# Gate and first feed-forward products of a decoder step in Strassen's form (Winograd's variant, one level)

## The chip, the cores and the metric

One core of one Trainium2 chip runs the whole program in one launch. The metric is the device time of that launch in microseconds (us). Before the change three runs gave 1571.78, 1574.46 and 1579.22 us; the median is 1574.46.

## The reference, cut to what matters

Two decoder layers are computed for 512 prompt tokens and 32 sample tokens together (544 columns, NT). In each layer, after the mixers and their output projection, this follows (D = 1024, inner width 4096):

```python
h = layer_norm(ALPHA * h + mix, ln1_g, ln1_b)
ff = jnp.square(jax.nn.relu(h @ w_ff1)) @ w_ff2
ple = jax.nn.sigmoid(h @ w_ple_gate) * (pe @ w_ple_proj)
h = layer_norm(ALPHA * h + ff + ple, ln2_g, ln2_b)
```

Everything is float32 at the interface. The change touches `h @ w_ple_gate` and `h @ w_ff1` and what lies around them.

## The kernel before, in words

**Numbers.** Each float32 operand of a large product is split into two parts of the format fp32r: `hi` is the operand rounded (a cast on ScalarE), `lo` is the operand less `hi` (a subtraction on VectorE or GpSimd). A product is then three matmuls per 128x128 weight block, weight-hi by x-hi, weight-lo by x-hi and weight-hi by x-lo (`mm3`; all matmuls have the one line L620).

**Tiling.** Activations are kept transposed: 8 blocks of 128 channels by 544 columns, in two halves of 288 and 256 columns (HALF). A gate or first-layer product of one output block (a "chunk" of weights, 128x1024 float32, 512 KB) is 2 halves x 8 blocks x 3 = 48 matmuls. The gate has 8 such chunks in a layer, the first feed-forward product (f1) 32, the second one (f2) 32.

**Order of the feed-forward part** (`backbone`): output projection `w_o` (second half of its contraction per column half), the projection `w_p`, the gate, then twice (kh = 0, 1): 16 chunks of f1 whose squared-ReLU results stay on chip as hi and lo, and 8 output blocks of f2 over those 16. The residual is added from the hi and lo parts of h in `evac_f2` (L1734, L1736).

**Weights on their way.** SyncE's queue loads a chunk into one of 2 `raw` buffers (L591); `splits` casts it to `hi` on ScalarE (L603) and makes `lo` on VectorE, for some chunks on GpSimd (L607); there are 4 `hi` and 4 `lo` buffers, freed when the chunk's products are issued.

**LayerNorm.** `ln_apply` adds sums over the channels by matmuls, works out mean and inverse root in a chain of small VectorE operations (L654), broadcasts both by matmuls and spawns `ln_col` for each of 8 blocks: two VectorE operations that read PSUM (L740, L742), a scale and bias on ScalarE (L748), the cast (L753) and GpSimd's subtraction (L755).

**Evacuation of f1** (`evac_f1`): ReLU on ScalarE (L1712), square on GpSimd (L1715), cast on ScalarE (L1717), lo on VectorE (L1719).

**Planner.** The program is written by generators ("streams") that a small planner, `Sched`, runs while the program is built: every step carries an engine and a charge in ns (`cP`, `cV`, `cA`, `cS`, `cG` for TensorE, VectorE, ScalarE, GpSimd), every buffer and event a planned time, and at each point the step with the earliest planned start, less its stream's priority (`PR`), is issued. An `Alt` lets the planner take the engine that ends earlier. So the order on each engine is fixed when the program is built. The chip runs each engine's list in order.

Of the kernel before, what the change touches and what calls it, by code (L numbers as in the profile page):

```python
# [23 lines left out]
T = 4  # L24
# [24 lines left out]
PR = {'q_sample': -1.5, 'free_raw': 7, 'gmix': 1.0, 'evac_c1': 10.5, 's_scores': 13.0, 's_block': 8.5, 'mix_b': 4.5, 'load_r': 6.5, 'kidx': 10.5, 's_attn': 14, 'evac_au': 6.5, 'head': 8.0, 's_kt': 10.0, 'loads': 1.5, 'evac_q': 0.0, 'sgu_load': 7.5, 's_relu': 12.5, 'mix_a': 13, 'setup1': 9.0, 's_attn_f': 8.5, 'gmlp': 7.5, 'unit': 8.0, 'load_pe': 14, 'evac_oa': 8, 'backbone': -2, 'evac_c0': -1.5, 'setup2': -2, 'splits': 7.5, 's_qk': 0.5, 'gnorm': 7.0, 'store': 11, 'setup': 3.0}  # L49
# [31 lines left out]
class Sched:  # L81
    def __init__(self, pools, caps):
# [6 lines left out]
        self.n = 0  # L89

# [24 lines left out]
    def run(self):  # L115
        while self.streams:
# [27 lines left out]
            for s in self.streams:  # L144
                if isinstance(s.item, (list, Alt)):
                    opts = s.item.opts if isinstance(s.item, Alt) else (s.item,)
                    bo = None
                    for i, o in enumerate(opts):
                        e, c = o[0]
                        st = max(s.ready + hop(s.e, e), self.eng.get(e, 0.0))  # L150
                        if bo is None or st + c + BIAS < bo[0]:
                            bo = (st + c, st - (WP if e == "P" else WO) * s.prio, i)
# [25 lines left out]
def cP(n, k=1):  # L178
    return ("P", max(n / 2.4 + 2.5, 107.0) * k)
# [193 lines left out]
def build(tc, I, O, cols):  # L373
# [4 lines left out]
    caps = {"Ah": 1, "Al": 1, "Bh": 1, "Bl": 1, "w": 5, "raw": 2, "hi": 4, "lo": 4, "u": 23, "t": 11, "mm": 2, "at": 6}  # L378
# [4 lines left out]
    S = Sched(pools, dict(caps, lk=1, un=UN))  # L383
# [142 lines left out]
    chunks = []  # L526

    def chunk(src, f, g=False, native=False, s=False, cut=()):
# [5 lines left out]
        chunks.append(c)  # L534
        return c

    W = []
    for l in range(L):
# [10 lines left out]
        w["g"] = [chunk(I["w_g"][l, c, 0], 1024, c < 2) for c in range(8)]  # L549
        w["f1"], w["f2"] = [None] * 32, [[None] * 4 for _ in range(8)]  # L550
        for kh in range(2):
            for c in range(16):
                w["f1"][kh * 16 + c] = chunk(I["w_f1"][l, kh * 16 + c, 0], 1024)
            for c in range(8):
                for k in range(2):
                    w["f2"][c][kh * 2 + k] = chunk(I["w_f2"][l, c, kh * 2 + k], 1024)
# [36 lines left out]

    def splits():
# [1515 lines left out]
```

## Time and profile before

| what | value |
|---|---|
| median of three runs | 1574.46 us |
| the profiled execution's own time | 1573.14 us |
| its span, first to last instruction | 1571.4 us |
| mean granted TensorE clock over the span | 0.974 of full speed |
| matmuls | 12598 |
| memory read and written | 156 and 6 MB |

The profile comes from one execution. "PE" is the matmul side of TensorE, "PEld" its weight loads, which overlap; DVE is VectorE, ACT ScalarE, POOL GpSimd, SP the queue that issues most transfers. Busy times of matmuls overlap and their ends are modelled, so the rate of a stretch is read from the starts or from the number of matmuls in it. A duration of DVE or POOL includes time in which the instruction had started and was held up. A row of the timeline begins with its start and its duration in us. In a row that groups instructions, the number after the bar is the summed busy time, then the mean of one in ns, then the idle time of that engine before them.

### The profile page before, as it was taken

To read this page: it belongs to the slowest core of one execution; us is meant where nothing else is said; L and a number is where in the kernel's file an instruction comes from. 1 tells how busy PE (TensorE), PEld (TensorE's weight loads), DVE (VectorE), ACT (ScalarE), POOL (GpSimd) and SP (SyncE) were. 2 spreads that over 40 slices of the span, in tenths; PEclk is the share of its full clock that TensorE was granted. 3 is DMA by queue.
4 is the path that set the end of the run, shared out by engine and by line. 5 is a ranking of instruction groups with operands and counts; after the bars stand their busy time and mean duration, and the time that the engine had idled before them with its cause. 6 is when DMAs were issued, how large, how long until landed. Compare 5 with 4: busy or idle time off the path is not lost.

```text
span 1571.4 us, 31307 instructions
## 1 busy us (share of the span) xinstructions
PE 1508.9 (96%) x12598; PEld 1429.5 (91%) x12598; DVE 844.6 (54%) x2114; ACT 700.5 (45%) x1593; POOL 469.0 (30%) x517
## 2 busy tenths in 40 slices
PE   8999889999999999999989989999999999999997
PEld 6788877999999999999967888779999999999997
DVE  5489985573333343333555899866633334433334
ACT  4677675363442124422355767554534421244222
POOL 3446731250331003311335357214403300133110
PEclk9999999999999999999989999999999999999997
DMA  7455424123222322222245543241232222322221
GB/s 233 159 175 158 134 70 136 50 74 108 82 94 68 103 87 94 82 94 81 79 137 169 174 141 134 77 142 49 69 107 94 82 82 81 108 81 94 68 81 58
DMA packets 55473, 164.48 MB, mean 105 GB/s; under 512 B 7648, under 2 KB 15008, under 8 KB 55328
## 3 DMA queue, kind: packets, MB, share of 16 engines
q1 hardware_dynamic: 44960, 124.73, 24.1%
q0 software_dynamic: 10368, 37.75, 7.4%
q8 instruction: 99, 1.62, 0.4%
q14 instruction: 46, 0.38, 0.1%
HBM read 156.09 MB, written 6.37 MB: 103 GB/s over the span
## 4 chain that ended last, share of the span: by engine, by line
PE 84%; DVE 9%; ACT 3%; issue 2%; DMA 1%; another core or an unknown queue 1%; POOL 0%; SPq 0%; ACTq 0%; DVEq 0%; POOLq 0%
PE mm L620 66%; PE at L620 14%; PE at L1383 1%; PE at L1470 1%; DVE u L1021 1%; DVE tmp L654 1%; DVE m L1019 1%; ACT maskb L1091 1%; DVE gy L654 1%; DVE c L1106 1%; DMA raw<-in_w_c 1%; DVE y L654 1%; PE at L1637 0%; DVE lo L607 0%
## 5 line engine op out<-in xcount | busy, mean ns | idle before, releaser
L603 ACT CAST hi<-raw 128x1024 fp32r<-128x1024 f32 (+1 forms) x201 | 206.3, 1028 | 315.9 <-PE mm L620 279.8
L620 PE MATMUL mm<-Bh,hi 128*128 128x288 f32 (+1 forms) x1040 | 304.5, 293 | 2.6 <-DVE t L797 2.5
L620 PE MATMUL mm<-Ah,hi 128*128 128x256 f32 (+1 forms) x1040 | 303.0, 291 | 0.4 <-DVE t L800 0.4
L620 PE MATMUL mm<-Bh,lo 128*128 128x288 f32 (+1 forms) x1040 | 302.7, 291 | 0.5 <-issue 0.4
L620 PE MATMUL mm<-Bl,hi 128*128 128x288 f32 (+1 forms) x1040 | 301.8, 290 | 0.4 <-issue 0.4
L620 PE MATMUL mm<-Ah,lo 128*128 128x256 f32 (+1 forms) x1040 | 301.6, 290 | 0.0
L620 PE MATMUL mm<-Al,hi 128*128 128x256 f32 (+1 forms) x1040 | 301.1, 289 | 0.0
L607 DVE TENSOR_TENSOR lo<-raw,hi 128x1024 fp32r<-128x1024 f32 (+4 forms) x171 | 204.7, 1205 | 165.6 <-ACT hi L603 165.4
L1715 POOL TENSOR_TENSOR t<-t 128x288 f32<-128x288 f32 (+1 forms) x128 | 128.7, 1005 | 536.8 <-ACT t L1712 478.0
L620 PEld LDWEIGHTS mm<-Bh,hi 128*128 128x128 f32 x1040 | 198.7, 191 | 4.8 <-issue 3.2
L620 PEld LDWEIGHTS mm<-Ah,hi 128*128 128x128 f32 x1040 | 197.5, 190 | 2.3 <-issue 1.9
L620 PEld LDWEIGHTS mm<-Bh,lo 128*128 128x128 f32 x1040 | 198.3, 191 | 0.7 <-issue 0.6
L620 PEld LDWEIGHTS mm<-Bl,hi 128*128 128x128 f32 x1040 | 197.9, 190 | 0.2 <-issue 0.2
L620 PEld LDWEIGHTS mm<-Ah,lo 128*128 128x128 f32 x1040 | 197.2, 190 | 0.2
L620 PEld LDWEIGHTS mm<-Al,hi 128*128 128x128 f32 x1040 | 196.7, 189 | 0.0
L1729 DVE TENSOR_TENSOR u<-u,mm 128x288 f32<-128x288 f32 (+1 forms) x64 | 28.0, 438 | 227.6 <-PE mm L620 227.6
L620 PE MATMUL mm<-w,hi 128*128 128x288 f32 (+1 forms) x576 | 125.1, 293 | 0.1
L696 POOL TENSOR_TENSOR u<-u,t 128x288 f32<-128x288 f32 (+1 forms) x48 | 44.3, 922 | 235.7 <-ACT t L689 235.6
L620 PE MATMUL mm<-u,hi 128*128 128x288 f32 (+1 forms) x512 | 107.2, 289 | 0.0
L620 PEld LDWEIGHTS mm<-w,hi 128*128 128x128 f32 x576 | 97.6, 192 | 0.3 <-issue 0.3
L607 POOL TENSOR_TENSOR lo<-raw,hi 128x1024 fp32r<-128x1024 f32 x30 | 71.6, 2385 | 55.0 <-ACT hi L603 45.8
L620 PEld LDWEIGHTS mm<-u,hi 128*128 128x128 f32 x512 | 84.8, 189 | 0.0
(354 smaller groups left out, 3108.9 us busy)
## 6 DMA issues: line engine op xcount, KB each, us to landing
raw<-in_w_f SPq DMA_DIRECT2D x128, 512.0 KB, 3.2
raw<-in_w_q SPq DMA_DIRECT2D x16, 512.0 KB, 3.2
raw<-in_w_o SPq DMA_DIRECT2D x16, 512.0 KB, 4.3
raw<-in_w_g SPq DMA_DIRECT2D x16, 512.0 KB, 3.2
raw<-in_w_au SPq DMA_DIRECT2D x8, 512.0 KB, 3.9
raw<-in_w_av SPq DMA_DIRECT2D x8, 512.0 KB, 3.2
u<-in_x SPq DMA_DIRECT2D x8, 272.0 KB, 2.7
u<-hD SPq DMA_DIRECT2D x8, 272.0 KB
```

What stands on the lines that cost most here:

```text
L603: A.copy(c.hi[:, a:b], c.raw[:, a:b])
L607: (G if c.g else V).tensor_tensor(c.lo[:, a:b], c.raw[:, a:b], c.hi[:, a:b].bitcast(F32), op=ALU.subtract)
L620: PE.matmul(out, l, r, start=start, stop=stop, skip_group_check=True)
L654: f(*args, **kw)
L696: G.tensor_tensor(st["s2"][:, a:b], st["s2"][:, a:b], sq[:, :n], op=ALU.add)
L1019: V.max(m8, work[:, :N])
L1021: V.match_replace(work[:, :N], m8, work[:, :N], -3.3e38)
L1091: A.activation(y.maskb, Iv, AF.Sign, scale=-1.0, bias=thr, accum_out=cf)
L1106: V.scalar_tensor_tensor(c, d, (2 ** (bit - 1)) if bit else 0, c, op0=ALU.bitwise_xor, op1=ALU.bitwise_xor)
L1383: PE.transpose(p[:, c * 128:(c + 1) * 128], P[:, c * 128:(c + 1) * 128], ident)
L1715: G.tensor_tensor(rl[:, :n], rl[:, :n], rl[:, :n], op=ALU.mult)
L1729: V.tensor_tensor(r[:, a:b], r[:, a:b], ps[:, :n], op=ALU.add)
```

## The change

The outputs of the gate and of f1 are made in pairs of chunks. The 256 outputs, the 1024 inputs and the 544 columns of a pair are each cut in two, and the product of the resulting 2x2 blocks is formed from 7 block products instead of 8: A11 B11, A12 B21, S2 T2, S1 T1, S3 T3, S4 B22 and A22 T4, where S1 to S4 are sums and differences of weight blocks (128x512 each, `wsum`) and T1 to T4 of column blocks of h (`mtee`). A block product is 4 blocks x 3 = 12 matmuls of 272 columns (NH). Three PSUM banks serve a pair; between block products the accumulating bank is read and the product goes on accumulating in it.

What else goes with it:

- Weight parts: for each pair A11 with A12 (1024 wide), S2, S1, S3, S4 and A22 (512 wide each) are split into hi and lo; a half-filled buffer holds A22. The sums are made on GpSimd or VectorE, as the planner finds.
- Activations: LN1 writes its float32 result back into `y.R`; `moving` and `mv` make hi and lo of B11, B21, B22 and T1 to T4. The residual is added from `y.R` in `fin_g`.
- f1's results are held for a quarter of the inner width: steps of 5, 4, 4 and 3 pairs (STEPS), each followed by an f2 pass over 8 blocks for all 8 outputs; a ring of 5 pairs holds hi and lo. The first two outputs of a pass share one loop over the blocks.
- 4 `raw` buffers instead of 2; the area of the software transfer queue's descriptors is set to 8192 bytes (`dynamic_dma_scratch_size`).
- The planner charges TensorE n/2.25 + 5.2 ns, knows a tiling mode of a group of matmuls and charges 95 ns for a change of it; all priorities are new.

```diff
+NH = NT // 2
+ST = 3
+RING = 5
+STEPS = ((0, 5), (5, 9), (9, 13), (13, 16))
...
+SWITCH = 95.0
...
-    return ("P", max(n / 2.4 + 2.5, 107.0) * k)
+    return ("P", max(n / 2.25 + 5.2, 107.0) * k)
...
-    caps = {"Ah": 1, "Al": 1, "Bh": 1, "Bl": 1, "w": 5, "raw": 2, "hi": 4, "lo": 4, "u": 23, "t": 11, "mm": 2, "at": 6}
+    caps = {"Ah": 1, "Al": 1, "Bh": 1, "Bl": 1, "w": 5, "raw": 4, "hi": 4, "lo": 4, "u": 23, "t": 11, "mm": 2, "at": 6}
...
+    PACKS = (("A11", "A12"), ("S2", "S1"), ("S3", "S4"), ("A22",))
...
+    def wsum(c, free):
...
+        for name, x, z, op, done_with in (("S1", a21, a22, ALU.add, ()), ("S2", "S1", a11, ALU.subtract, (0,)),
+                                          ("S3", a11, a21, ALU.subtract, (0, 1)), ("S4", a12, "S2", ALU.subtract, (0,))):
+            tok = yield Al("st", None)
+            t = yield Al("u", U)
+            E = V if (yield Alt([cG(512)], [cV(512)])) else G
...
+            E.tensor_tensor(t[:, :512], get(x), get(z), op=op)
...
+    def wsplit(c, names, src, hi, lo, ready):
+        n = 512 * len(names)
+        yield ready
+        x = src()
+        yield [cS(n)]
+        A.copy(hi[:, :n], x)
+        E = G if (yield Alt([cV(n)], [cG(n)])) else V
+        E.tensor_tensor(lo[:, :n], x, hi[:, :n].bitcast(F32), op=ALU.subtract)
...
+    def wino3(c, M, fin, early):
+        T, (_, e1, e2, e3, e4) = c.T, c.e
+        pb = yield Al("at", [128, 512])
+        yield from wprod(c, "S2", pb, M["T2"], True, False)
+        S.spawn(wadd(T, "u2", pb, e1, e2), 11)
+        pg = yield Al("at", [128, 512])
+        yield from wprod(c, "S1", pg, M["T1"], True, False)
+        S.spawn(wcopy(T, "s5", pg, e3), 11)
+        if not early:
+            yield from wino2(c, M, fin)
+        yield e2
+        yield from wprod(c, "S3", pb, M["T3"], False, False)
+        S.spawn(wadd(T, "u3", pb, e2, e4), 11)
+        S.spawn(wout22(T, fin, (e3, e4)), 10)
+        yield e3
+        yield from wprod(c, "S4", pg, M["B22"], False, True)
+        S.spawn(wout(T, "u2", pg, fin, 0, 1), 10)
+        yield e4
+        yield from wprod(c, "A22", pb, M["T4"], False, True)
+        S.spawn(wout(T, "s1", pb, fin, 1, 0), 10)
...
+    def sub(n, out, x, z):
+        E = G if (yield Alt([cV(n)], [cG(n)])) else V
+        E.tensor_tensor(out, x, z, op=ALU.subtract)
...
+            if th == 0:
...
+                A.activation(t[:, :NH], src[:, :NH], AF.Relu)
...
+                E = V if (yield Alt([cG(NH)], [cV(NH)])) else G
+                E.tensor_tensor(t[:, :NH], t[:, :NH], t[:, :NH], op=ALU.mult)
+            else:
+                yield [cV(NH)]
+                V.scalar_tensor_tensor(t[:, :NH], t[:, :NH], 0.0, t[:, :NH], op0=ALU.max, op1=ALU.mult)
+            hi, lo = act(y, k)
+            yield [cS(NH)]
+            A.copy(hi[:, sl], t[:, :NH])
+            yield from sub(NH, lo[:, sl], t[:, :NH], hi[:, sl].bitcast(F32))
...
+            for p in range(2):
+                yield from wino1(g[p], y.M)
+            for p in range(2):
+                yield from wino2(g[p], y.M, fg[p])
+            for p in range(2):
+                yield from wino3(g[p], y.M, fg[p], True)
+            for p in range(2, 4):
+                yield from wino(g[p], y.M, fg[p])
...
-    nc = bacc.Bacc("TRN2", target_bir_lowering=False, num_devices=1)
+    nc = bacc.Bacc("TRN2", target_bir_lowering=False, num_devices=1, dynamic_dma_scratch_size=8192)
```

## Rows read from the trace of the kernel before

**Rows 1.** The page's first part: busy us, share of the span, instructions.
```profile
PE 1508.9 (96%) x12598; PEld 1429.5 (91%) x12598; DVE 844.6 (54%) x2114; ACT 700.5 (45%) x1593; POOL 469.0 (30%) x517
```
**Rows 2.** Windows: stretch, length, busy us of PE, PEld, DVE, ACT, POOL (instructions), clock, DMA.
```profile
120.00:160.00 40.00, 37.01 (x404) 33.53 (x404) 39.31 (x133) 30.30 (x94) 25.37 (x23) 1.00 0.51 161
...
400.00:440.00 40.00, 40.00 (x320) 40.00 (x320) 14.27 (x21) 16.56 (x33) 14.05 (x14) 1.00 0.28 93
...
520.00:560.00 40.00, 40.00 (x318) 40.00 (x317) 17.66 (x28) 6.71 (x7) 0.00 (x0) 1.00 0.27 87
```
**Rows 3.** Chain that ended last, merged pieces: start us, us, what.
```profile
20.44 8.26 DMA raw<-in_w_c
...
356.06 407.84 PE mm L620 x3234
...
789.63 3.19 DMA raw<-in_w_au
...
1134.24 407.39 PE mm L620 x3234
```
**Rows 4.** Timeline, f1 of layer 0: first matmul of two successive chunks.
```profile
416.37 0.30 PE L620 MATMUL mm<-Bh,hi 128*128 128x288 f32 x1
...
422.41 0.30 PE L620 MATMUL mm<-Bh,hi 128*128 128x288 f32 x1
```
**Rows 5.** Groups by form in 380 to 480 us: element-wise work of f1.
```profile
L607 DVE TENSOR_TENSOR lo<-raw,hi 128x1024 fp32r<-128x1024 f32 x17 | 20.8, 1226 | 33.2 <-ACT hi L603 33.2
...
L603 ACT CAST hi<-raw 128x1024 fp32r<-128x1024 f32 x17 | 17.8, 1048 | 23.2 <-PE mm L620 23.2
L1715 POOL TENSOR_TENSOR t<-t 128x288 f32<-128x288 f32 x15 | 10.0, 668 | 56.4 <-ACT t L1712 43.6 <-DVE Al L1719 6.4 <-DVE w L1719 3.6
...
L1719 DVE TENSOR_TENSOR Al<-t,Ah 128x256 fp32r<-128x256 f32 x8 | 3.4, 426 | 7.5 <-ACT Ah L1717 7.5
L1717 ACT CAST Ah<-t 128x256 fp32r<-128x256 f32 x8 | 3.2, 406 | 11.9 <-POOL t L1715 11.9
```
**Rows 6.** Timeline of DVE and POOL around 317 and 417 us.
```profile
317.06 2.41 POOL L607 TENSOR_TENSOR lo<-raw,hi 128x1024 fp32r<-128x1024 f32 x1
317.62 0.45 DVE L742 TENSOR_TENSOR t<-t,at 128x288 f32<-128x288 f32 x1
...
317.99 0.45 DVE L740 TENSOR_TENSOR t<-u,at 128x288 f32<-128x288 f32 x1
...
318.35 1.40 DVE L694 TENSOR_TENSOR u<-u,u 128x256 f32<-128x256 f32 x1
...
417.65 1.23 DVE L607 TENSOR_TENSOR lo<-raw,hi 128x1024 fp32r<-128x1024 f32 x1 [1.82 <-ACT hi L603]
...
417.98 1.37 POOL L1715 TENSOR_TENSOR t<-t 128x256 f32<-128x256 f32 x1 [3.10 <-ACT t L1712]
```
**Rows 7.** Chain, 316 to 362 us: LN1 of layer 0, second half, then gate.
```profile
328.44 2.28 DVE y L654
...
334.26 0.68 PE at L620 x4
...
337.25 18.81 PE at L620 x150
```
**Rows 8.** Waits of PE in 0 to 360 us (us in total, times, longest): first and last.
```profile
PE at L620 <- ACT maskb L1091: 5.5, 6, 1.8
...
PE at L1383 <- DVE u L1379: 0.6, 1, 0.6
```
**Rows 9.** Waits of SP's queue, longest first.
```profile
SPq L591 <- DVE lo L607: 787.7, 141, 31.0
```
**Rows 10.** Chain, 250 to 270 us: its longest piece.
```profile
259.36 4.85 another core or an unknown queue
```

More of the change, by code (lines that the diff above doesn't have):

```diff
@@ L534, in chunk, with wchunk @@
         chunks.append(c)
+        if not native:
+            splitq.append(c)
+        return c
+    class Wino:
+        pass
+    def wchunk(src0, src1, queue=True):
+        c = Wino()
+        c.raws = (chunk(src0, 1024, native=True), chunk(src1, 1024, native=True))
+        c.ev = {b: Ev() for b in WB}
+        c.hl = {}
+        c.left = [4, 3]
+        if queue:
+            splitq.append((c, PACKS))
         return c
@@ new lines, in wdrop @@
+    def wdrop(c, name):
+        c.S[name][1] -= 1
+        if c.S[name][1] == 0:
+            S.free(c.S[name][0])
+            S.free(c.S[name][2])
+    def wsplit(c, names, src, hi, lo, ready):
[6 more added lines that the diff above has]
+        E.tensor_tensor(lo[:, :n], x, hi[:, :n].bitcast(F32), op=ALU.subtract)
+        for name in names:
+            if name[0] == "S":
+                wdrop(c, name)
+            S.set(c.ev[name])
+        if names[0] == "A11":
+            wraw(c, 0)
+        if names[0] == "A22":
+            wraw(c, 1)
@@ L613, in splits, with wprod @@
                 S.set(re)
+    def wprod(c, name, ps, mov, start, stop):
+        hi, lo, slot = c.hl[name]
+        yield c.ev[name]
+        for i in range(4):
+            mh, ml, me = mov[i]
+            yield me
+            if i % 2 == 0:
+                yield [cP(NH, 6)]
+            mm3(ps[:, :NH], hi[:, i * 128:i * 128 + 128], lo[:, i * 128:i * 128 + 128], mh, ml,
+                start and i == 0, stop and i == 3)
+        slot[2] -= 1
+        if slot[2] == 0:
+            S.free(slot[0])
+            S.free(slot[1])
@@ new lines, in wcopy, with wadd, wout @@
+    def wcopy(T, name, ps, ev):
+        T[name] = yield Al("t", [128, 288])
+        yield from copy(T[name][:, :NH], ps[:, :NH], NH)
+        S.set(ev)
+    def wadd(T, name, ps, need, ev):
+        yield need
+        T[name] = yield Al("t", [128, 288])
+        yield [cV(NH)]
+        V.tensor_tensor(T[name][:, :NH], T["s1"][:, :NH], ps[:, :NH], op=ALU.add)
+        S.set(ev)
+    def wout(T, name, ps, fin, ci, th):
+        t = T[name]
+        yield [cV(NH)]
+        V.tensor_tensor(t[:, :NH], t[:, :NH], ps[:, :NH], op=ALU.add)
+        S.free(ps)
+        yield from fin(ci, th, t, None)
@@ new lines, in wout22, with wino1 @@
+    def wout22(T, fin, need):
+        for e in need:
+            yield e
+        t, z = T["u3"], T["s5"]
+        E = V if (yield Alt([cG(NH)], [cV(NH)])) else G
+        E.tensor_tensor(t[:, :NH], t[:, :NH], z[:, :NH], op=ALU.add)
+        S.free(z)
+        yield from fin(1, 1, t, None)
+    def wino1(c, M):
+        c.T = {}
+        c.e = [Ev() for _ in range(5)]
+        c.pa = yield Al("at", [128, 512])
+        yield from wprod(c, "A11", c.pa, M["B11"], True, False)
+        S.spawn(wcopy(c.T, "s1", c.pa, c.e[1]), 11)
@@ new lines, in fin_g, with fin @@
+    def fin_g(y, p):
+        def fin(ci, th, t, ps):
+            c = 2 * p + ci
+            sl = slice(th * NH, th * NH + NH)
+            src = t
+            if t is None:
+                t = yield Al("t", [128, 288])
+                src = ps
+            yield [cA(NH)]
+            A.activation(t[:, :NH], src[:, :NH], AF.Tanh, scale=0.5)
+            if ps is not None:
+                S.free(ps)
+            for e in y.proj[c]:
+                yield e
+            r = y.R2[c][:, sl]
+            yield [cV(NH)]
+            V.scalar_tensor_tensor(r, t[:, :NH], 1.0, r, op0=ALU.add, op1=ALU.mult)
+            S.free(t)
+            yield [cV(NH)]
+            V.scalar_tensor_tensor(r, y.R[c][:, sl], ALPHA, r, op0=ALU.mult, op1=ALU.add)
+            S.set(y.gd[c][th])
+            y.gcnt[c] += 1
+            if y.gcnt[c] == 2:
+                S.free(y.R[c])
+        return fin
@@ L1725, in evac_f2 @@
+    def evac_f2(y, q, c, half, ps, st):
         a, b = HALF[half]
@@ new lines, in backbone @@
+            st2 = {}
+            for q, (p0, p1) in enumerate(STEPS):
+                for p in range(p0, p1):
+                    if p == 4:
+                        ts = []
+                        for _ in range(4):
+                            t = yield Al("u", U, F32R)
+                            ts.append(t)
+                        held += ts
+                        y.ring.append([(ts[0], ts[1]), (ts[2], ts[3])])
+                    yield from wino(w["f1"][p], y.M, fin_f1(y, p))
+                if q == 3:
+                    for t in y.xtra:
+                        S.free(t)
```

320 lines of the change are left out of this document (204 added, 116 removed).

## The prediction, made before the result was known

> **What bounds the kernel now.** I read the page's busy shares first, then the windows of 40 us, the chain, the groups, and last the timeline of single stretches. TensorE (PE) is busy in 96% of the span, VectorE (DVE) in 54% and GpSimd (POOL) in 30% [rows 1]. The windows show two kinds of stretch. In the feed-forward part (356 to 764 us, and again from 1134) each 40 us hold about 320 matmuls at full granted clock, with DVE and POOL near 14 us of the 40 in f1, and DVE at 17.7 with POOL at 0 in f2; in the mixers DVE is full (39.3 of 40) beside PE [rows 2]. The chain agrees: two pieces of 407 to 408 us are nothing but matmuls, 3234 each [rows 3]. So in the part that the change touches PE is the only bound, and fewer matmuls are worth their full price as long as DVE and POOL, which gain the work that PE loses, stay beside it. That condition is the question.
>
> **Removed from PE.** A chunk of f1 starts 6.04 us after the one before [rows 4]: 48 matmuls of 288 and 256 columns, 126 ns each on average. The new ones have 272 columns, the same mean, so I keep 126 ns. A pair of chunks was 96 matmuls (12.08 us) and becomes 7 x 12 = 84 (10.57 us): 1.51 us less. There are 4 gate and 16 f1 pairs in a layer, 40 in all: **-60.4 us**. f2 keeps its matmuls (8 outputs x 2 halves x 32 blocks x 3). Its 32 additional adds per layer replace the 32 residual operations that leave `evac_f2`; both are DVE operations of 256 or 288 columns, and f2 leaves DVE more than half idle [rows 2]: nothing.
>
> **Added to DVE and POOL, f1.** Durations: two inputs in SBUF cost DVE 0.43 us at 256 and 1.23 at 1024 columns [rows 5], so by interpolation 0.44 at 272 and 0.69 at 512. Back to back one starts about 0.08 earlier than the last one's end (0.37 apart at 0.45 each) [rows 6]; I count 0.36, 0.61 and 1.15. A pair now asks for lo parts 1.15 + 5 x 0.61 = 4.2; weight sums 4 x 0.61 = 2.4; activation lo's 4 x 0.36, squares 4 x 0.36 and one output sum 0.36 = 3.2; and four adds that read PSUM, 4 x 0.36 = 1.4. Together 11.3 us if all is DVE's, against 10.57 of PE; before it was 3.7 us of DVE and four POOL squares. So POOL must take some, and it costs about 2 us for each us of DVE (2.41 against 1.15 at 1024, 0.67 against 0.37 at 288) [rows 5, 6].
>
> What the planner's charges don't hold is that the two engines exclude each other. A POOL square that starts while DVE subtracts two SBUF tensors lasts 1.37 instead of 0.67 and ends 0.47 after DVE does; a DVE sum of two SBUF tensors lasts 1.40 where such a one takes 0.43, because POOL's 2.41 us subtraction is running; the DVE operations beside it with one input in PSUM keep their 0.45 [rows 5, 6]. So DVE's two-SBUF work and POOL's work add up on one clock; only the 1.4 us of PSUM adds can lie beside POOL. If POOL takes p us, that clock needs 9.9 + p/2 per pair: 11.4 for p = 3, 12.4 for p = 5, 13.4 for p = 7. The planner takes the engine that it thinks ends earlier, weight sums go to POOL at a tie, and it sees DVE overfull; I take p = 5.
>
> The Trainium skill (SBUF — State Buffer, section Who interferes with whom) states the same as a rule: a VectorE instruction with two SBUF inputs and a GpSimd instruction that reads SBUF share one read port, and whichever issues second waits for the whole of the other. The trace agrees (1.37 against 0.67, 1.40 against 0.43). Were it a mere sharing of bandwidth, POOL's 5 us would hide beside DVE and the stall below would be near nothing; by the rule it is the 12.4.
>
> So DVE and POOL fall behind by about 12.4 - 10.6 = 1.8 us per pair. They have a lead: a freed hi/lo buffer pair (S2, S1, after three products, 4.5 us into the pair) takes the next pair's first part, ready some 2.5 us later (cast 1.05, lo 1.23) [rows 5], 3.5 us before PE needs it. The first pair of a step is prepared during f2. A step of n pairs thus loses (n - 1) x 1.8 - 3.5: 3.7, 1.9, 1.9 and 0.1 us, 7.6 per layer, 15 in all (0 at p = 3, 39 at p = 7). Besides, PE's A22 product waits for a DVE read of the bank that S3 has filled, with only S4 (1.5 us) for cover. The read takes some 0.7 with its signals; a 1.23 us subtraction or a held-up operation ahead of it on DVE makes PE late by up to 0.5 or more. I take 0.2 for each of 40 pairs, 7 us (0 to 20). Together **+22 us** for f1, bounds 0 and 60. ScalarE has 1.05 + 5 x 0.6 + about 8 x 0.4 = 7.3 us per pair [rows 5] and stays beside PE.
>
> **Added around LN1 and the gate.** LN1's second half is broadcast at 334.3 and the gate starts at 337.3 [rows 7]. The gate's first four block products (6.0 us) need B11 and B21, from the first half; from 343 on the products need T2, T1, T3, B22, T4, each from both halves. Before, the first half's gate products covered 9 us, and nothing more than a cast and a POOL subtraction stood behind LN1. Between 334 and the end of the first two pairs (337.3 + 21.1 = 358.4, 24 us) DVE now has 16 LN operations at 0.36 (5.8), 44 subtractions for T and the lo's (15.8) and two pairs' weights and sums (2 x 8.4, less 2.3 made before: 14.6): 36.2 us, and the gate's own 16 last steps (5.8) that may come later. Beside the PSUM operations POOL can take about 9 us, which relieves DVE by 4 to 5. So 32 us of work stand against 24: 8 late per layer. Late parts are needed late (T4 last), the deferred steps and the other two pairs' own excess fall on top; I take 8 per layer, **+16 us**, bounds 0 (all of B11 and B21 done in the first half's shadow) and 36. Small chains on DVE suffer too: one operation of LN1's chain already waited 2.28 us behind POOL [rows 7].
>
> **Outside.** Two more `raw` buffers let SP issue earlier: most of SP's waiting for a buffer is for DVE's lo (788 us in sum), without PE being late in the steady part [rows 9, 3]. On the chain two weight loads stand, 8.3 us at the start and 3.2 at layer 1 [rows 3]; at most 11 can go, I take -4. Priorities and the mode charge reorder the mixers: PE's listed waits there, 13 kinds from 5.5 down to 0.6 us, make 26 us per layer [rows 8], so an order can win or lose some 20 in all; I take 0. The smaller descriptor area concerns POOL's gathers; the one long wait for an unnamed queue is 4.85 us [rows 10], and I bound that edit by 0 and +10 and take 0.
>
> **Sum**, against the profiled execution's own 1573.1 us (1.7 outside its span, 1.3 under the median of the runs): 1573.1 - 60.4 + 22 + 16 - 4 = **1547 us**.
>
> **Rivals.** *PE stays the bound* (chance 0.25). DVE has 26 of 40 us free in f1 now [rows 2], and if POOL gets 3 us a pair or less, the lead covers the deficit. Stalls of 10 us leave 1573 - 60 + 10 - 4 = 1519 (1505 to 1532). Against it: 11.3 us of DVE work on 10.57. *The saving is eaten up* (0.15): stalls of 50 to 65 us, p near 7 in f1 and the upper bound at the gate: 1566 to 1582. *Slower: DVE and POOL take turns and set the pace* (0.16). With p = 7 a pair after the first of its step takes 13.4 us instead of 10.57: 24 pairs x 2.8 less 8 leads of 3.5 is 40 us; held-up reads before A22 cost 0.5 x 40 = 20; the gate costs 36 and its last two pairs 2 x 2 x 2.8 = 11. 1573 - 60 + 107 = 1620, or 1582 to 1625 in parts. It decides once the stalls pass 1.5 us per pair, PE's own gain. For it speak the pairwise exclusion and charges without it; against it that each step starts with a lead and f2 lets DVE catch up. *The forecast* (1532 to 1566) has 0.44.
>
> A difference of 0.5% (8 us) is about what can be told from no change. Faster by more: 0.25 + 0.44 = 0.69; within: 0.15; slower: 0.16. The range 1508 to 1595 leaves out the lowest part of the first rival and most of the last one's upper half, under 0.2.
>
> **What would show it.** Matmuls fall by 480 to about 12118, and starts stay 126 ns apart in f2 and in a pair's products. In f1 windows DVE goes from 14 to above 30 of 40 us, POOL to above 15, with POOL groups whose means are well above their free duration. PE's waits name DVE (the reads before A22) and lo parts of the weights; a late third and fourth pair in each step, the first one prompt. Between 337 and 360 PE waits for the lo's of T2 to T4. The steps fail if pairs run at 10.6 us throughout (exclusion costs nothing), or if the first pair of a step is as slow as the last (no lead). The whole is wrong if mixers move by more than 20 us, or 272 columns take clearly more than 126 ns.

## The result and the profile after

The changed kernel takes 1641.97 us (median of 4 runs, 1637.94 to 1643.95), the kernel before 1576.45 on the same chip: ratio 1.0416 [1.0381, 1.045]. It is slower, against a forecast of 1547. The profiled execution took 1641.4 us, with a span of 1639.7 and a mean granted clock of 0.954.

The page's first part after, beside [rows 1]:

```profile
PE 1489.8 (91%) x12118; PEld 1400.4 (85%) x12118; DVE 1216.0 (74%) x2671; ACT 763.4 (47%) x1752; POOL 612.5 (37%) x609
```

The 480 matmuls are gone, and TensorE is idle for 150 us of the span where it was idle for 62. The windows after (stretch, length, busy us of PE, PEld, DVE, ACT, POOL, granted clock, DMA share, GB/s) stand beside [rows 2]; 449.0 to 462.3 is one pair of f1:

```profile
120.00:160.00 40.00, 34.11 (x312) 25.67 (x314) 37.39 (x135) 26.54 (x74) 26.57 (x27) 0.87 0.65 227
360.00:400.00 40.00, 26.54 (x160) 24.72 (x159) 39.72 (x55) 18.30 (x44) 28.53 (x23) 0.83 0.19 66
400.00:440.00 40.00, 35.63 (x275) 34.68 (x275) 37.74 (x61) 16.87 (x34) 19.61 (x14) 1.00 0.24 80
449.00:462.30 13.30, 11.07 (x86) 10.63 (x85) 12.50 (x19) 6.23 (x13) 6.37 (x6) 1.00 0.25 81
520.00:560.00 40.00, 38.49 (x305) 38.05 (x304) 27.99 (x44) 14.56 (x29) 10.96 (x10) 1.00 0.17 56
```

In the gate (360 to 400) half of the 320 matmuls are left, and DVE has no free time; in f1 a pair takes 13.3 us for its 84 matmuls, and DVE is nearly as full (12.5 us). The granted clock takes part in the gate. It falls to the lower of its two levels (0.50, 1.2 GHz) while PE waits 3.71 us for an operand, and matmuls then start 0.23 us apart instead of 0.13. PE's rows there (start, us) and two windows:

```profile
369.43 0.82 PE L808 MATMUL at<-w,hi 128*128 128x272 f32 x2 [3.71 <-DVE w L1898]
...
373.13 0.43 PE L808 MATMUL at<-Bh,hi 128*128 128x272 f32 x1
373.36 0.43 PE L808 MATMUL at<-Bh,lo 128*128 128x272 f32 x1
...
377.26 0.29 PE L808 MATMUL at<-Bh,hi 128*128 128x272 f32 x1
377.39 0.28 PE L808 MATMUL at<-Bh,lo 128*128 128x272 f32 x1
```
```profile
368.80:375.60 6.80, 5.95 (x24) 5.63 (x25) 6.51 (x14) 4.16 (x12) 3.73 (x5) 0.50 0.01 4
375.60:392.70 17.10, 11.26 (x84) 10.41 (x82) 17.10 (x21) 6.71 (x14) 12.37 (x9) 1.00 0.26 92
```

PE's waits over the whole span (us in total, times, longest), beside [rows 8]:

```profile
PE at L808 <- DVE t L747: 46.6, 41, 4.2
PE at L808 <- DVE y L842: 13.3, 4, 4.3
PE at L808 <- ACT maskb L1280: 10.4, 8, 3.1
PE at L808 <- ACT t L848: 8.9, 8, 1.4
PE at L808 <- DVE w L1898: 8.2, 4, 4.1
```

The first one is the read of the accumulating bank between two block products (`wadd`), waited for 41 times. The timeline of one f1 pair, DVE and then POOL (start, us), beside [rows 6], shows why DVE is late:

```profile
450.08 0.68 DVE L672 TENSOR_TENSOR lo<-u,hi 128x512 fp32r<-128x512 f32 x1
450.68 1.52 DVE L1898 TENSOR_TENSOR Al<-t,Ah 128x272 fp32r<-128x272 f32 x1
452.13 1.77 DVE L650 TENSOR_TENSOR u<-raw 128x512 f32<-128x512 f32 x1
...
456.03 0.42 DVE L747 TENSOR_TENSOR t<-t,at 128x272 f32<-128x272 f32 x1
```
```profile
450.25 1.66 POOL L672 TENSOR_TENSOR lo<-u,hi 128x512 fp32r<-128x512 f32 x1 [1.69 <-ACT hi L670]
451.87 1.48 POOL L672 TENSOR_TENSOR lo<-raw,hi 128x512 fp32r<-128x512 f32 x1
...
455.75 0.86 POOL L2016 TENSOR_TENSOR t<-t 128x272 f32<-128x272 f32 x1 [0.19 <-ACT t L2012]
```

Follow the ends. POOL's first runs to 451.91, and DVE's subtraction of 272 columns, started at 450.68, ends 0.29 after that. POOL's second starts at 451.87 and ends at 453.35; DVE's weight sum, started at 452.13, ends 0.55 after that. The two engines take turns. The read of PSUM at 456.03 keeps its 0.42 beside POOL.

Where the 68.3 us of the span went, from the starts of instructions (us):

| stretch | before | after | difference |
|---|---|---|---|
| mixers, layers 0 and 1 (to the last `evac_o`) | 321.3, 320.6 | 335.1, 334.4 | +27.6 |
| from there to the first gate matmul | 16.5, 17.2 | 22.0, 21.0 | +9.3 |
| gate, to the first f1 matmul | 48.3, 48.3 | 65.4, 65.9 | +34.7 |
| f1 and f2, to the last `evac_f2` | 392.0, 391.5 | 388.3, 388.7 | -6.5 |
| tail | 15.6 | 18.8 | +3.2 |

### The profile page after: what moved, and what is told of

It reads as the page before. It is cut to its first block, busy times and chain, and to the rows that moved or that the text cites. A ratio compares the mean times of both kernels' runs of the same rounds, so it can differ in the third digit from the quotient of the medians.

```text
span 1639.7 us, 31266 instructions
## 1 busy us (share of the span) xinstructions
PE 1489.8 (91%) x12118; PEld 1400.4 (85%) x12118; DVE 1216.0 (74%) x2671; ACT 763.4 (47%) x1752; POOL 612.5 (37%) x609
## 5 line engine op out<-in xcount | busy, mean ns | idle before, releaser
L808 PE MATMUL at<-w,hi 128*128 128x272 f32 (+1 forms) x864 | 204.2, 300 | 58.9 <-DVE t L747 46.6
L808 PEld LDWEIGHTS at<-w,hi 128*128 128x128 f32 x864 | 150.4, 193 | 70.0 <-DVE t L747 55.6
L808 PE MATMUL mm<-Ah,hi 128*128 128x288 f32 (+1 forms) x504 | 150.4, 298 | 1.4 <-DVE u L1873 1.4
L808 PE MATMUL mm<-Bh,hi 128*128 128x288 f32 (+1 forms) x504 | 149.5, 297 | 2.2 <-DVE u L1873 1.4
L808 PE MATMUL at<-w,lo 128*128 128x272 f32 (+1 forms) x512 | 149.7, 292 | 0.0
L808 PE MATMUL mm<-Ah,lo 128*128 128x288 f32 (+1 forms) x504 | 148.8, 295 | 0.7 <-POOL lo L715 0.7
L808 PE MATMUL mm<-Al,hi 128*128 128x288 f32 (+1 forms) x504 | 148.2, 294 | 0.0
L808 PE MATMUL mm<-Bh,lo 128*128 128x288 f32 (+1 forms) x504 | 146.7, 291 | 0.0
L808 PE MATMUL mm<-Bl,hi 128*128 128x288 f32 (+1 forms) x504 | 146.5, 291 | 0.0
L715 DVE TENSOR_TENSOR lo<-raw,hi 128x1024 fp32r<-128x1024 f32 (+5 forms) x95 | 116.9, 1231 | 19.3 <-ACT hi L711 18.5
L670 ACT CAST hi<-raw 128x1024 fp32r<-128x1024 f32 (+1 forms) x80 | 66.6, 832 | 79.1 <-PE mm L808 29.9
```

Source lines behind the costliest of these rows:

```text
L670: A.copy(hi[:, :n], x)
L715: (G if c.g else V).tensor_tensor(c.lo[:, a:b], c.raw[:, a:b], c.hi[:, a:b].bitcast(F32), op=ALU.subtract)
L808: PE.matmul(out, l, r, start=start, stop=stop, skip_group_check=True)
```

## The experiments

The stretches of all kernels, in the order of the text. "Feed-forward" is the three middle rows above together.

| kernel | ratio to before, 95% | mixers 0, 1 | feed-forward 0, 1 | tail |
|---|---|---|---|---|
| before | 1 | 321.3, 320.6 | 456.8, 457.1 | 15.6 |
| after | 1.0416 [1.0381, 1.045] | 335.1, 334.4 | 475.7, 475.6 | 18.8 |
| b_scratch | 0.9989 [0.9967, 1.0011] | 326.9, 321.8 | 456.8, 456.4 | 15.2 |
| a_bank | 1.043 [1.0404, 1.0457] | 339.1, 337.0 | 475.9, 475.7 | 18.8 |
| a_dve | 1.0082 [1.0062, 1.0102] | 331.5, 334.0 | 446.9, 446.9 | 21.3 |
| a_lock | 1.0277 [1.0238, 1.0316] | 335.8, 349.8 | 448.9, 449.1 | 21.3 |
| b_pr | 1.0194 [1.0177, 1.0211] | 335.1, 321.8 | 467.6, 466.2 | 14.9 |
| b_chg | 1.063 [1.0601, 1.0658] | 363.8, 359.0 | 457.0, 459.5 | 15.7 |
| b_raw4 | 1.005 [1.0034, 1.0066] | 314.8, 320.0 | 456.8, 458.1 | 15.0 |
| a_oldpr | 1.0806 [1.0763, 1.0849] | 367.7, 357.1 | 472.4, 473.1 | 19.0 |
| a_dve_oldpr | 1.048 [1.0454, 1.0505] | 369.2, 355.2 | 447.6, 447.0 | 21.2 |
| a_oldall | 1.037 [1.0344, 1.0396] | 315.5, 345.9 | 472.2, 471.2 | 20.3 |
| a_dve_oldall | 1.0304 [1.0275, 1.0333] | 313.5, 339.9 | 468.1, 465.8 | 20.7 |
| a_dve_oldpr_ws | 1.0553 [1.0516, 1.0591] | 368.8, 360.1 | 452.0, 452.3 | 21.2 |
| h_dve | 1.0011 [0.9987, 1.0035] | 333.7, 336.9 | 439.7, 440.5 | 21.3 |
| h_fit | 0.9845 [0.9812, 0.9878] | 326.0, 336.1 | 432.2, 431.3 | 19.3 |
| a_fit | 1.0168 [1.0131, 1.0205] | 341.3, 332.3 | 447.6, 448.9 | 18.8 |
| b_fit | 1.0114 [1.0091, 1.0137] | 337.9, 329.5 | 455.6, 455.2 | 15.3 |
| **h_mix** | **0.9738 [0.9702, 0.9774]** | 319.3, 333.9 | 429.5, 429.8 | 19.1 |

Kernels whose names begin with a_ are the changed kernel with an edit, those with b_ the kernel before with an edit, those with h_ a mixture. "The gate" in the text runs from its first matmul to the first one of f1.

The stretches come from one profiled execution each, and those of the mixers differ between runs of one order, at another granted clock. The mixers of layer 0 in the kernel before, b_scratch (which has the same order), the changed kernel and b_pr (the clock is the first figure behind POOL's):

```profile
0.00:321.30 321.30, 296.38 (x2680) 257.75 (x2681) 235.42 (x737) 195.01 (x507) 138.38 (x167) 0.96 0.42 138
0.00:326.90 326.90, 305.39 (x2681) 266.64 (x2682) 235.54 (x738) 195.88 (x508) 141.04 (x167) 0.93 0.42 135
0.00:335.10 335.10, 308.92 (x2676) 272.36 (x2677) 240.74 (x743) 193.74 (x509) 135.81 (x166) 0.91 0.41 136
0.00:335.10 335.10, 301.05 (x2674) 257.15 (x2675) 238.77 (x740) 190.97 (x503) 132.72 (x165) 0.95 0.41 132
```

One and the same order gives 321.3 at 0.96 and 326.9 at 0.93, so a difference of some 6 us in the mixers of one run is not to be read. The changed kernel has 0.91 there: a part of its 13.8 us may be clock rather than order, and no run separates the two.

### Two suspects that were none

b_scratch, the descriptor area alone, in the kernel before:

```diff
-    nc = bacc.Bacc("TRN2", target_bir_lowering=False, num_devices=1)
+    nc = bacc.Bacc("TRN2", target_bir_lowering=False, num_devices=1, dynamic_dma_scratch_size=8192)
```

> The kernel before with one edit, the descriptor area of software transfers at 8192 bytes. The mixers of the changed kernel take about 13.8 us longer in each layer. If the smaller area holds up POOL's gathers, this kernel takes some 20 to 28 us more than before (1595 to 1604) with the loss in the mixers. If the order (priorities, charges) costs it, nothing changes: within 6 us of before.

Measured 1574.07, ratio 0.9989: no cost.

a_bank gives A22 a PSUM bank of its own, so that it no longer waits for the read of what S3 left:

```diff
...
-        yield e4
-        yield from wprod(c, "A22", pb, M["T4"], False, True)
-        S.spawn(wout(T, "s1", pb, fin, 1, 0), 10)
+        pd = yield Al("at", [128, 512])
+        yield from wprod(c, "A22", pd, M["T4"], True, True)
+        S.spawn(wout21(T, pd, fin, e4), 10)
...
```

> The changed kernel with a PSUM bank of its own for the A22 product, so that PE need not wait until DVE has read the bank that S3 filled. Handshake theory (the wait itself costs, 1.1 us per steady pair): f1's steady pair falls from 13.3 to about 12.2, total 1610 to 1625. DVE-bound theory: the stall moves to another place of the pair, a pair stays at 13.0 to 13.4, total within 8 us of the changed kernel.

Measured 1644.64, ratio 1.043. The gaps between matmuls in f1, both layers together, stay at 47 us and only move: in the changed kernel they lie before or in S3 (22.8), A22 (19.0) and A12 (5.5), in a_bank in S3 (35.8), A12 (9.3) and S4 (2.4). So the read of this bank does not set the pace; DVE, which makes it late, is left as the suspect.

### VectorE without GpSimd beside it

a_dve puts each free choice of the gate and of f1 on VectorE; shown is the edit in `wsum`, and the same is done in `wsplit`, `wout22`, `fin_f1` and `sub`:

```diff
-            E = V if (yield Alt([cG(512)], [cV(512)])) else G
+            yield [cV(512)]
+            E = V
```

> The changed kernel with every choice between GpSimd and VectorE in the new gate and f1 code settled for VectorE (weight sums, lo parts, squares, the last output sum). Exclusion theory: POOL's 5.4 us per pair cost more than the 2.7 us of DVE that they spare, because the two shut each other out; a steady f1 pair falls from 13.3 to 11.3 to 11.8 us, f1's stalls from 45 to about 20 us, total 1600 to 1625. Rival, DVE simply has too much work and needs POOL's help: a steady pair rises to 14 us or more, total 1650 to 1680.

Measured 1587.02, 55 us faster than the changed kernel; the direction is as expected, the gain is larger. f1 with f2 falls from 388.3 to 369.3 us per layer, and most pairs take 10.6. The groups of DVE in f1, first of the changed kernel (435 to 476), then of a_dve (420 to 456), after the bar busy us and mean ns:

```profile
L1898 DVE TENSOR_TENSOR Al<-t,Ah 128x272 fp32r<-128x272 f32 x10 | 9.9, 993 | 1.9 <-ACT Ah L2022 1.9
L672 DVE TENSOR_TENSOR lo<-u,hi 128x512 fp32r<-128x512 f32 x9 | 7.5, 829 | 0.0
L650 DVE TENSOR_TENSOR u<-raw 128x512 f32<-128x512 f32 x3 | 5.3, 1774 | 0.0
...
L747 DVE TENSOR_TENSOR t<-t,at 128x272 f32<-128x272 f32 x6 | 2.5, 424 | 0.0
```
```profile
L674 DVE TENSOR_TENSOR lo<-u,hi 128x512 fp32r<-128x512 f32 x12 | 8.0, 676 | 0.0
L1902 DVE TENSOR_TENSOR Al<-t,Ah 128x272 fp32r<-128x272 f32 x13 | 5.4, 427 | 0.0
...
L651 DVE TENSOR_TENSOR u<-raw 128x512 f32<-128x512 f32 x3 | 2.0, 675 | 0.0
```

The same subtraction takes 427 ns alone and 993 beside POOL. In the changed kernel POOL's help cost DVE more than it took off it. But the gate gains nearly nothing (65.4 to 63.3); it only begins earlier, 14.3 us behind the mixers instead of 22.0. The windows of a_dve, gate and one stretch of f1:

```profile
337.00:409.00 72.00, 54.26 (x409) 53.11 (x408) 69.54 (x167) 37.74 (x83) 0.00 (x0) 0.88 0.19 59
432.00:444.00 12.00, 12.00 (x96) 11.85 (x95) 12.00 (x27) 6.88 (x16) 0.00 (x0) 1.00 0.27 89
```

Behind LN1 DVE is busy for 69.5 of 72 us with POOL at nothing: the stage from LN1 to the first f1 matmul has DVE work for all its time. PE's longest waits are for weight parts that come late, the longest (17.1 us) in the gate's first pair:

```profile
PE at L811 <- DVE lo L674: 40.6, 8, 17.1
```

a_lock keeps POOL, but the planner knows that POOL's work and DVE's work on two SBUF inputs (`cT`) exclude each other:

```diff
+                        if shared(o[0]):
+                            st = max(st, self.eng.get("X", 0.0))
...
-    return ("G", (2.1 * n + 148.0) * k)
+    return ("G", (2.1 * n + 148.0) * k, 0, 1)
...
+def cT(n, k=1):
+    return ("V", (n / 0.96 + 70.0) * k, 0, 1)
```

> The changed kernel with a planner that knows the exclusion: every POOL element-wise step and every DVE step marked as having two SBUF inputs also holds one shared resource in the plan. Nothing else is changed, and the planner still may give steps to POOL. Exclusion theory: the planner leaves nearly all of the gate's and f1's steps on DVE, a steady f1 pair falls from 13.3 to 10.6 to 11.6 us, total 1585 to 1610, near the kernel with all on DVE (1587). Rival (POOL's slow steps, not the exclusion, were mis-charged): POOL keeps most of its 5.4 us per pair, total within 15 us of the changed kernel.

Measured 1611.43, just above the range, ratio 1.0277: f1 with f2 369.2, the same as a_dve; gate 63.8. The planner now leaves POOL little (6.3 of the 54 us from 416 to 470), and the feed-forward part is repaired as far by knowledge as by leaving POOL out; the mixers of layer 1 got 15 us longer with the new order, and that is most of what keeps it behind a_dve.

### The mixers: charges and priorities

b_pr is the kernel before with the new priority table and nothing else (names that only the changed kernel has are not used):

```diff
-PR = {'q_sample': -1.5, 'free_raw': 7, 'gmix': 1.0, 'evac_c1': 10.5,
+PR = {'q_sample': 7.0, 'free_raw': 1.5, 'gmix': 1.0, 'evac_c1': 14.5,
...
```

> The kernel before with the new priority table alone (old products, old charges, old buffers). If the priorities make the mixers slow: +15 to +30 us, evac_o's last start of layer 0 near 335 instead of 321 us. If the descriptor area or the new charges do it: within 8 us of before.

Measured 1606.28, ratio 1.0194: layer 0's mixers take 335.1 us with none of the new products. That this is the changed kernel's figure is chance as far as the runs show, for its charges are others and its clock there is lower. Layer 1's stay (321.8). In both layers the feed-forward part is 9 to 11 us longer, in the plain gate above all (57 to 58 us, where the kernel before has 48.3).

One long chain of layer 0 can be followed by a single line, the threshold search (31 steps on ScalarE, each waiting for the one before). Before, after, b_chg (below) and b_pr: ns shortest, median, longest, then first and last start in us.

```profile
L1091 ACT ACTIVATE maskb<-u,c x31: 711/728/738, 80.9 to 190.0; 128x513 bf16<-128x513 f32 x31
```
```profile
L1280 ACT ACTIVATE maskb<-u,c x31: 714/728/765, 137.2 to 233.5; 128x513 bf16<-128x513 f32 x31
```
```profile
L1105 ACT ACTIVATE maskb<-u,c x31: 712/727/755, 136.3 to 242.7; 128x513 bf16<-128x513 f32 x31
```

```profile
L1091 ACT ACTIVATE maskb<-u,c x31: 711/728/742, 71.6 to 174.3; 128x513 bf16<-128x513 f32 x31
```

Each step takes the same; after the change the chain starts 56 us later and ends 44 later, and in b_chg too it is late. A tempting story, but b_pr contradicts it: there the search starts earlier than before, and the mixers are as long as after. That the table makes layer 0 of the kernel before longer is shown; at which chain it does so is not.

b_chg is the other half, all of the new TensorE charges and the mode charge under the old table (left out below: lower charges for the groups of small tiles, 900 ns for 1000 and the like):

```diff
-    return ("P", max(n / 2.4 + 2.5, 107.0) * k)
+    return ("P", max(n / 2.25 + 5.2, 107.0) * k)
...
+                        if e == "P" and mode(o[0]) != self.mode:
+                            st += SWITCH
...
```

> The kernel before with the new TensorE charges and the charge for a change of tiling mode, old priorities, old products. If a priority table only fits the charges for which it was chosen: the mixers go astray as in the changed kernel with old priorities (evac_o of layer 0 from 335 us or later instead of 293), total 1600 to 1680. If the new charges are harmless and only the new priorities cost: within 8 us of before.

Measured 1659.56, ratio 1.063, mixers 363.8 and 359.0: the new charges (9% higher per matmul, 126 against 116 ns at 272 columns, besides the mode charge and those left out) cost 98 us under a table chosen for the old ones. For a matmul the new charge is the truer one, since matmuls do start 126 ns apart; the order got worse all the same.

b_raw4 has 4 `raw` buffers and the small descriptor area:

```diff
-    caps = {"Ah": 1, "Al": 1, "Bh": 1, "Bl": 1, "w": 5, "raw": 2, "hi": 4, "lo": 4, "u": 23, "t": 11, "mm": 2, "at": 6}
+    caps = {"Ah": 1, "Al": 1, "Bh": 1, "Bl": 1, "w": 5, "raw": 4, "hi": 4, "lo": 4, "u": 23, "t": 11, "mm": 2, "at": 6}
```

> The kernel before with 4 weight buffers instead of 2 (and the smaller descriptor area that makes room for them, which by itself did nothing). If earlier loads help: 2 to 8 us less than before. If they only shift the plan: between 5 us less and 20 us more, with the difference in the mixers.

Measured 1569.15 against 1561.96, ratio 1.005. Layer 0's mixers are 6.5 us shorter in its profiled run than in that of the kernel before, about as much as two runs of one order differ by above; the medians show no gain, but 7 us more.

Four runs put old tables back into the changed kernel: a_oldpr the old priorities for the old streams, a_dve_oldpr the same with VectorE alone, a_oldall and a_dve_oldall also the old charges.

```diff
-PR = {'q_sample': 7.0, 'free_raw': 1.5, 'gmix': 1.0, 'evac_c1': 14.5,
+PR = {'q_sample': -1.5, 'free_raw': 7, 'gmix': 1.0, 'evac_c1': 10.5,
...
-    return ("P", max(n / 2.25 + 5.2, 107.0) * k)
+    return ("P", max(n / 2.4 + 2.5, 107.0) * k)
...
```

> The changed kernel with the priorities of before for every stream that was there before; the ten new streams keep theirs. If the new priorities make the mixers 13 us longer in each layer (evac_o's last start of layer 0 at 335 instead of 321 us), these come back to within 4 us of before and the total falls to 1605 to 1625. If the new charges, the mode charge or the buffers do it: total within 8 us of the changed kernel.

> Both edits: gate and f1 choices all on DVE, and the priorities of before for the streams that were there before. If the two losses are separate, they add up: 1587 less 20 to 30, so 1555 to 1568, faster than before. If the mixers' loss is no matter of priorities: 1580 to 1590.

> The changed kernel with the charges and the priorities of before together (the ten new streams keep theirs). If table and charges belong together: the mixers come back to within 8 us of before in each layer (evac_o of layer 0 from 293 to 301 us), total 1610 to 1630. If the new streams and buffers disturb the mixers by themselves: evac_o from 305 us or later, total 1640 or more.

> As the one above, with all of the gate's and f1's choices on DVE. If both causes are found and add up: 1555 to 1570, below before. If the mixers don't come back: 1580 to 1640.

Measured 1694.51, 1644.28, 1620.29 and 1609.41. The first two are misses: the old priorities under new charges give mixers of 368 and 369 us in layer 0, 357 and 355 in layer 1. With both old, layer 0 is back at 315.5 and 313.5. So the old table holds for the charges that it was chosen with and not for the new ones, with the new products (a_oldpr) and without (b_chg). No run has the new table and the new charges together in the kernel before. Layer 1's mixers stay at 340 to 346, longer than in the changed kernel (334.4).

Nor do the causes add up, as the last expectation hoped: under the old charges the feed-forward part with all on VectorE takes 468.1 and 465.8 us, against 446.9 under the new ones (a_dve), with a gate of 71.5 and 69.2. The old charges serve the mixers of layer 0, the new ones the Strassen products.

a_dve_oldpr_ws raised one priority more, that of `wsplit`, to bring the late weight parts forward: 1658.06, ratio 1.0553, 14 us more than a_dve_oldpr and so outside both expectations.

```diff
-'wsplit': -2.5
+'wsplit': 9.0
...
```

> As the kernel with both edits, and the weight splits' priority at 9 instead of -2.5. With all on DVE PE waited 18 us in each layer for the weight lo part of the gate's first pair. If that is order, not DVE's capacity: 8 to 15 us less per layer than the kernel with both edits, 1530 to 1550. If DVE is simply full between LN1 and the gate: the wait moves to the lo parts of h, total within 8 us of it.

The wait moves to the operands of h, as the second expectation had it; of a_dve_oldpr_ws:

```profile
PE at L811 <- DVE Bl L1902: 13.1, 2, 7.4
```

The gate stays at 63.0 (62.9 in a_dve_oldpr), while f1 with f2 goes from 370.7 to 375.0: with DVE full, this order only chooses what is late.

### Plain gate, Strassen f1

h_dve is a_dve with the gate's 8 chunks as plain products again, on the same column blocks of 272; B12 lies in T1's buffer until the gate is issued:

```diff
-            for p in range(2):
-                yield from wino1(g[p], y.M)
...
+            for cs in ([0, 1, 2], [3], [4], [5], [6], [7]):
+                for th in range(2):
...
+                        mh, ml, me = y.M[("B11", "B12", "B21", "B22")[2 * (k // 4) + th]][k % 4]
...
+            S.set(y.xal["T1"])
```

> The version with all of the change's free choices on VectorE (1587, ratio 1.008), but the gate in 8 plain products again (48 matmuls per chunk, on the same column blocks of 272), and only f1 in Strassen form; the T1 operand is stored after the gate, because its buffer holds B12 until then. Theory (VectorE is full behind LN1, and the gate suffers because its Strassen products need T1 to T4 at once; with plain products these have the gate's 48 us to be made in): gate 63 down to 49 us per layer, f1 with f2 stays at 369 to 374, so 28 less at most: 1559 to 1570, ratio 0.990 to 0.997. Rival (the VectorE debt is only carried over to the first pairs of f1): gate 49, f1 with f2 383, total 1585 to 1590, ratio 1.007 to 1.010.

Measured 1573.06, ratio 1.0011 [0.9987, 1.0035]: level with the kernel before, 11 us (0.7%) better than a_dve. Both expectations missed. f1 with f2 takes 367.1, so the debt is not carried over to f1, as the rival would have it; but the gate takes 56.6, not 49. Here is what is left, PE's wait and DVE's list in 351 to 357:

```profile
PE at L809 <- DVE lo L715: 12.4, 2, 6.2
```
```profile
351.43 4.31 DVE L1900 TENSOR_TENSOR Bl<-u,Bh 128x272 fp32r<-128x272 f32 x12
355.65 1.22 DVE L715 TENSOR_TENSOR lo<-raw,hi 128x1024 fp32r<-128x1024 f32 x1
```

Twelve operand subtractions stand ahead of the `lo` of a gate chunk: an order again. b_pr, with the same table, has a plain gate of 57 to 58 too, and h_fit below, with another table and planner, 48.3.

h_fit, a_fit and b_fit have the planner of a_lock (VectorE's operations on one SBUF input marked too), and each a priority table fitted to its own kernel by trying tables on the planner. h_fit has the plain gate and Strassen f1, a_fit both in Strassen's form, b_fit neither. Of h_fit's edit (the new table's own line is left out):

```diff
+                        if shared(o[0]):
+                            st = max(st, self.eng.get("X", 0.0))
...
-PR = {'q_sample': 7.0, 'free_raw': 1.5, 'gmix': 1.0, 'evac_c1': 14.5,
...
```

> Plain gate, Strassen f1, GpSimd or VectorE chosen by a planner that knows that GpSimd's work and VectorE's work on two SBUF inputs exclude each other, and a priority table fitted to this kernel by trying tables on the planner. Theory (the mixers' 27 us are an order fitted badly, not a cost of the products): mixers near 321 us per layer as before, gate 49, f1 with f2 369 to 375: 1530 to 1550, ratio 0.973 to 0.985. Rival (a table fitted on the planner does not hold on the chip, since its charges leave out stalls): mixers of 330 to 350 us again, total 1560 to 1600, ratio 0.992 to 1.017.

> The changed kernel with the same planner (it knows the exclusion) and a priority table fitted to it in the same way; the gate stays in Strassen form. Theory: gate 60 to 64 us per layer, f1 with f2 369 to 372, mixers near 321: 1555 to 1575, ratio 0.99 to 1.00. Rival as for the run before: mixers of 330 to 350, 1590 to 1630, ratio 1.01 to 1.035.

> Control: the kernel before (no Strassen products) with the same planner, 4 raw buffers and a priority table fitted to it in the same way. If fitting on this planner gives mixers as good as before's, 1555 to 1575, ratio 0.99 to 1.00. If fitted tables do not hold on the chip, mixers of 330 to 350 us and 1595 to 1640, ratio 1.015 to 1.045; the two runs before are then to be read against this one, and not against the kernel before.

Measured 1546.5, 1597.49 and 1591.34 against 1570.58. h_fit's ratio is in its theory's band, by the feed-forward part: gate 48.3, f1 with f2 366. Its mixers (326.0, 336.1) are the rival's in layer 1. b_fit's 1.0114 lies between its two expectations; with mixers of 338 and 330, it shows that a table fitted on the planner does not of itself give the order of before. As the control it also prices the products, on one planner and one chip, each kernel with its own table: Strassen f1, with what goes with it, makes the program 45 us shorter (1546.5 against 1591.34), Strassen f1 and gate together 6 us longer (1597.49). The Strassen gate costs some 16 us of feed-forward per layer against the plain one (447.6 and 448.9 against 432.2 and 431.3): 8 in the gate, 2 to 4 before it, 6 in f1 with f2.

h_mix joins the two: in the mixers the old charges, the old priorities and no exclusion, from the gate to the end of f2 those of h_fit.

```diff
+        return PR.get(n, self.p0) if PH[0] else PRM.get(n, self.p0 if n in PRD else PR.get(n, self.p0))
...
+            PH[0] = 1
             xi = 2 * l + 1
...
+            PH[0] = 0
             for t in held:
```

> The feed-forward part of the run with ratio 0.9845 (plain gate, Strassen f1, the planner knows the exclusion), and in the mixers the old TensorE charges, the old priorities and no exclusion in the planner: the planner changes its tables at the gate and back at the end of f2. Theory (an order belongs to the charges and priorities it was chosen with, and the mixers' loss has nothing to do with the products): layer 0's mixers 315 us, as in the two runs that had the old tables and 4 raw buffers (314.8 and 315.5); layer 1's 320 to 335, since the feed-forward part now hands over otherwise; feed-forward 432 per layer and a tail of 19: 1518 to 1533, ratio 0.966 to 0.976. Rival (what the Strassen part leaves behind, buffers and loads, spoils layer 1's mixers): they take 340 to 350 us as with the old tables before, 1540 to 1550, ratio 0.98 to 0.987, no gain on the last version.

Measured 1534.42 (1527.51 to 1536.15) against 1573.7, ratio 0.9738 [0.9702, 0.9774], in the theory's band (the time itself is just above it), the fastest of all. The chain of waits of h_mix through the first part of f1 and f2 of layer 0 is matmuls again, as in [rows 3]:

```profile
387.20 61.92 PE at L827 x490
449.12 36.28 PE mm L827 x288
485.40 54.36 PE at L827 x432
539.76 36.20 PE mm L827 x288
```

One piece begins where the one before ends, and 490 matmuls in 61.92 us are 126 ns each. The windows, beside [rows 2]:

```profile
400.00:440.00 40.00, 40.00 (x320) 40.00 (x319) 39.60 (x81) 25.67 (x52) 4.09 (x4) 1.00 0.36 121
520.00:560.00 40.00, 40.00 (x320) 40.00 (x319) 23.98 (x42) 11.52 (x15) 0.00 (x0) 1.00 0.36 119
```

320 matmuls in 40 us, as before, but 84 do what 96 did; DVE is 99% busy and just keeps up. What remains against the kernel before is layer 1's mixers (333.9, the upper end of the theory's band) and the tail (19.1). Why layer 1's mixers are longer with Strassen products in each run that has the old tables (334 to 346 against 320) was not settled.

## Why the prediction was wrong, step by step

**Removed from PE, -60.4: right.** 12118 matmuls as foretold; a pair without stalls takes 10.6 us (a_dve, h_fit, h_mix), and f1 with f2 then falls by 26 us per layer, of which the removed matmuls are 24.

**f1, +22: the term was mis-sized; gaps between matmuls are 47 us** (the 16 pairs of a layer take 193 us where 16 x 10.57 is 169). The mechanism, DVE and POOL on one clock, is what the timeline shows, and in part the shape: the first pair of a later step runs in 10.6, the second in 12.6, the third in 13.3; but the last one of a step takes 10.9, where the prediction had it late. By an estimate from the shortest durations that POOL has for such operations in the trace (1.26 us at 512 columns, 0.64 to 0.78 at 272), its share in the pair shown was 5.3 us, about the 5 assumed. But a steady pair took 13.3, not 12.4, and the first step has no lead (its first four pairs take 13.2 to 13.3), where the prediction gave each step one. The wait before A22, put at 7 us for all 40 pairs, came to 19 in f1 alone, and the larger one before S3 (22.8) the prediction did not have. f1 and f2 gained 6.5 us instead of 26.

**LN1 and gate, +16: mis-sized most; gaps in the gate are 47 us, and it starts 9 us later besides, both layers together.** The estimate set 32 us of DVE work against 24 for the first two pairs and let the rest come later. In fact DVE has work for 70 us up to the first f1 matmul (a_dve's window), so nothing "later" was free. Some 9 of the 47 are a term that the prediction did not have: about 90 gate matmuls of the two layers start 0.23 us apart, at the lower clock level behind PE's waits. The upper bound of 36 is passed as well. Other orders helped little: with the old table and charges the gate takes 65.9 (a_oldall). And from the end of layer 0's mixers to f1 the Strassen gate takes 87.4 us in the changed kernel, and still 77.6 with POOL out (a_dve), 79.7 in a_lock and 75.7 in a_fit (whose shorter gate begins later), against 64.8 in the kernel before. So about 10 of the 22 us per layer go with POOL's share; the rest, 11 to 15, stays in each of these versions, with DVE full.

**Outside, "I take 0": the step that failed.** The mixers take 27.6 us more, and by the prediction's own sign, mixers that move by more than 20, the whole is wrong. In layer 0 the planner's order can do this: the new table alone makes it 335.1 in the kernel before (b_pr), and the old table with the old charges brings the changed kernel back to 315.5 (a_oldall). How much of the 13.8 is clock is open. The bound of 20 for what an order can do, taken from PE's listed waits [rows 8], was no bound: orders moved a layer's mixers by up to 48 us, since an order makes new waits, and those listed are only the ones that the present order has. The cause of layer 1's 13.8 stays open: the table alone leaves it at 321.8 (b_pr), and the old table and charges make it 345.9 (a_oldall).

**The raw buffers' -4** did not come: b_raw4, with the buffers alone, took 7 us more than the kernel before; why is not shown. **The descriptor area's 0** is right (b_scratch).

The rival on the slow side, DVE and POOL taking turns (0.16, up to 1625), named the right mechanism. It set the stalls at up to 107 us, where 94 came (47 and 47), and left the mixers alone, which is why the time lies above its 1625. The sum of the misses against the forecast: mixers 28, gate and before it 40, f1 20, tail and buffers 7.

## What to carry to other kernels

Before work is moved from a full engine to two others, ask whether these two can run side by side; here VectorE, with two operands in SBUF, and GpSimd could not, and leaving GpSimd idle made the changed kernel 55 us faster. Take a saving where the engine that pays for it has slack over the whole stage: the same Strassen form gave 26 us per layer in f1, and in the gate, where splitting the operands behind LayerNorm already fills VectorE, it lost 16. And treat a priority table and the charges that it was chosen with as one thing: the old table lost 98 us in the kernel before once the charges were new (b_chg). Change neither for a part of the program that works.

## What the runs showed of the hardware

Beside POOL a DVE operation on two SBUF operands is held up until POOL's instruction has ended: 1.77 us for a sum that takes 0.68, 1.52 for a subtraction that takes 0.43. The Trainium skill (SBUF — State Buffer, section Who interferes with whom) has this as a rule, that the second waits for the whole of the first; the trace agrees (the ends lie 0.29 and 0.55 us behind POOL's). What I had not expected is how much it makes over a stretch: the mean of a DVE subtraction more than doubles (993 against 427 ns). And the granted clock fell to 0.83 in the gate's window (360 to 400), where PE started half of 320 matmuls and its longest wait was 4.2 us, and was 1.00 in f1, where a steady pair has two stalls of 1.1 to 1.5 us. In the mixers the same order took 321.3 us at a mean of 0.96 and 326.9 at 0.93. The kernel before took 1562 to 1576 us (medians) beside the versions compared with it, so a version is judged by its ratio on its own chip.
